# Small loads ordered behind large ones, late steps of an expert stage moved to earlier blocks, and a normalization's statistics in a pool of their own

## The chip, the cores and the metric

One core of one Trainium2 chip runs the whole layer. The metric is the device time of one execution in microseconds (us), the median of several runs. TensorE is written PE (its weight loads PEld), VectorE DVE, ScalarE ACT, GpSimd POOL, and SyncE, which only issues DMAs here, SP. L and a number is a line of the kernel before.

## The reference, cut to what matters

One decoder layer on 256 tokens of 1024 features: an RWKV-7 token mixer, then a top-4-of-32 mixture of experts, then a gated per-layer embedding, each followed by a LayerNorm of `alpha * x + sublayer(x)`.

```python
x = layer_norm(ALPHA * x + rwkv7_time_mix(x, ...), ln_mix_g, ln_mix_b)
# moe_ffn: logits -> top 4 of 32 experts per token, softmax gates; per expert e:
    hcat = xb @ w_gu[e] + b_gu[e]                       # 1024 -> 2 * 1024
    glu, lin = min(hcat[:, :F], 7), clip(hcat[:, F:], -7, 7)
    act = glu * sigmoid(1.702 * glu) * (lin + 1)
    out = act @ w_down[e] + b_down[e]                   # 1024 -> 1024, weighted by the gate
x = layer_norm(ALPHA * x + ffn, ln_ffn_g, ln_ffn_b)
ple = (p @ ple_w_proj) * sigmoid(x @ ple_w_gate + ple_b_gate)
x = layer_norm(ALPHA * x + ple, ln_ple_g, ln_ple_b)
```

Everything is float32. The expert weights alone are 32 x (8 MB + 4 MB) in HBM, and each is read once.

## The kernel before, in words

The first part (the token mixer and the router) fills about the first quarter of the span. Then comes the expert stage, `Moe.experts`, and then `Moe.tail`, which does the two last LayerNorms and the embedding.

**The ring.** The weights come through `Ring`, eleven slots of 2 MB in SBUF. `weights` writes out by hand the order in which they are loaded, `ring.plan`. The 32 experts are taken in 16 blocks b of two experts 2b and 2b+1, and a block has twelve loads of 2 MB: four of `w_gu` for the first expert, four for the second, two of `w_down` for each. I call them (b,0) to (b,11). When PE has used up a slot, `ring.free` calls `add`, which fills the slot with the next entry of the plan. So the load that is added lies one ring ahead of the one that was freed. After the last block come `wg(0)` and `wg(1)`, the weights of the embedding's gate, each in four pieces; the two `w_down` loads of expert 31 are also in four pieces each.

At entry `2 * READY - 2` (in experts; READY is 8, so before block 7) stand two entries of another kind: `ple` loads `ple_w_proj` (1 MB) and keeps its slot to the end, and `norms` only keeps a slot, into which rows are later spread over all partitions. From there on the ring has nine slots.

**Small loads.** `ring.small` is a list of loads of 4 to 64 KB that are not issued at once: each `add` takes one from it. The `ple` entry puts nine there (four pieces of `p`, four LayerNorm rows, one row `ple_b_gate`). Each even block b up to 12 puts six there: the biases of four experts, from `biases`, into the tile `raw`. In the next odd block `parts` (L1076 to L1084) splits `raw` into three bf16 parts, with two casts on ACT and three instructions on DVE, which stand behind the activation of expert 2b. All loads are issued by SP, in one order. The order of instructions on each engine comes from a scheduler that models the time of each; a small load needs no slot to come free, a large one does, and nothing ties the two together.

**A block on PE**: `gu(2b)`, `gu(2b+1)` (the products with `w_gu`, tile `ph`, L1262, closed by four bias matmuls L1210), `combine(b-1)` (tile `acc`, L1323), one step of `ready` (b from 8 to 14, seven steps that prepare the embedding and the rows; the last four are tile `pn`, L1409), the transposes `tr` (tile `ptr`, L1285) and `gates`, in even blocks from 2 on `gather(2b+2)` (tile `pg`, L1229, which picks the tokens of the next four experts into `xq`), and `down` for both experts (tile `pd`, L1310). The last block (15) has its `combine(14)` between its two `gu`, and closes with `combine(15)`, which for each half cp of the tokens adds to `acc[cp]` and then starts the embedding's product (tile `tpg`, L1330).

**The tail.** `norm(0)` takes the statistics of `acc[0]` on DVE (tile `f_st`, L1505), then `turn(0)` transposes on PE (tile `tpt`, L1520), `product(0, ...)` multiplies with `wg` (tile `tpg`, L1529); meanwhile `norm(1)` runs on DVE. Tile `f_st` lies in the tail's pool `tw`, which is opened where the experts' pool `mw` was.

Of the kernel before, what the change touches and what calls it, by code (L numbers as in the profile page):

```python
# [11 lines left out]
F32 = mybir.dt.float32  # L12
# [9 lines left out]
E = 32  # L22
KC = D // 128
# [46 lines left out]
def ln_stats(nc, pool, x, st=None):  # L70
    if st is None:
        st = pool.tile([128, 2, 6], F32, name="ln_st", bufs=2)
        for h in range(2):
            nc.vector.bn_stats(st[:, h, :], x[:, h * 512:(h + 1) * 512])
    mv = pool.tile([128, 2], F32, name="ln_mv", bufs=2)
    nc.vector.bn_aggr(mv, st)
    rs = pool.tile([128, 1], F32, name="ln_rs", bufs=2)
    rsqrt1(nc, pool, rs, mv[:, 1:2], LN_EPS)
    return mv[:, 0:1], rs
# [6 lines left out]
class Ring:  # L86


    def __init__(self, nc):
        self.nc, self.plan, self.at, self.where, self.views, self.small = nc, [], 0, {}, {}, []  # L90

    def open(self, tc, ctx):
        for i in range(RING1):
# [16 lines left out]
    def add(self, tile_):  # L110
        if self.at < len(self.plan):
            key, fill = self.plan[self.at]
            self.at += 1
            self.views[key] = fill(self.nc, tile_)
            self.where[key] = tile_

            if self.small:
                self.small.pop(0)()

    def __getitem__(self, key):  # L120
        return self.views[key]
# [2 lines left out]
        self.add(self.where[key])  # L124


def weights(A, small):

    def gu(e, i):
        def fill(nc, t):  # L130
            v = t.rearrange("p (a b) -> p a b", b=2 * D)
            nc.sync.dma_start(v, A["moe_w_gu"][0][e].rearrange("(p c) f -> p c f", c=KC)[:, 2 * i:2 * i + 2, :])  # L132
            return v
        return ("gu", e, i), fill

    def down(e, i):
        def fill(nc, t):
            v = t.rearrange("p (a b) -> p a b", b=D)
            src = A["moe_w_down"][0][e].rearrange("(h q c) d -> h q c d", h=2, c=4)[i]
            n = 4 if e == E - 1 else 1  # L140
            for k in range(n):
                ks = slice(4 // n * k, 4 // n * (k + 1))
                nc.sync.dma_start(v[:, ks], src[:, ks])
            return v
        return ("d", e, i), fill

    def ple(nc, t):
        nc.sync.dma_start(t[:, 0:2048].rearrange("p (c d) -> p c d", c=2), A["ple_w_proj"][0].rearrange("(p c) d -> p c d", c=2))
        def later(out, in_):
            small.append(lambda: nc.sync.dma_start(out, in_))  # L150
        for cp in range(2):
            o = t[:, 3072 + 256 * cp:3328 + 256 * cp]
            later(o[0:64], A["p"][0, 0, cp * 128 + 64:cp * 128 + 128, :])
            later(o[64:128], A["p"][0, 0, cp * 128:cp * 128 + 64, :])
        for i, nm in enumerate(["ln_ffn_g", "ln_ffn_b", "ln_ple_g", "ln_ple_b"]):
            later(t[i:i + 1, 2048:3072], A[nm])
        later(t[32:33, 2048:3072], A["ple_b_gate"])
        return t

    def wg(i):  # L160
        def fill(nc, t):
            v = t.rearrange("p (a b) -> p a b", b=D)
            src = A["ple_w_gate"][0].rearrange("(p c) d -> p c d", c=KC)
            for k in range(4):
                nc.sync.dma_start(v[:, k, :], src[:, 4 * i + k, :])
            return v
        return ("wg", i), fill

    plan = []
    for e in range(0, E, 2):  # L170
        if e == 2 * READY - 2:
            plan += [("ple", ple), ("norms", lambda nc, t: t)]
        plan += [gu(e + j, i) for j in range(2) for i in range(4)]
        plan += [down(e + j, i) for j in range(2) for i in range(2)]
    return plan + [wg(0), wg(1)]
# [831 lines left out]
OFF0 = 1  # L1007
OFF1 = 0
PL = 4
READY = 8  # L1010


class Moe:
# [160 lines left out]
    def experts(self, ring):  # L1174


        tc, nc, c, x1, acc = self.tc, self.tc.nc, self.c, self.x1, self.acc
        ident, gate = c["ident"], self.gate
        with ExitStack() as ctx:
            W = ctx.enter_context(tc.tile_pool(name="mw", bufs=1, side="right", reuse_waits="tile"))  # L1180
            PS = self.mps.enter_context(tc.tile_pool(name="mps", bufs=1, space=bass.MemoryType.PSUM, reuse_waits="tile"))
            xq = W.tile([128, KC, 4 * CAP], F32, name="xq")
# [36 lines left out]
            def gather(e):  # L1219
                _, oh, _ = batch(e)  # L1220
                n = min(4, E - e)
                for cp in range(2):
                    self.places(oh, e, cp)
                for q in range(KC // 2):
                    pg = bank("pg").rearrange("p (k t) -> p k t", k=2)
                    for k in range(2):
                        for cp in range(2):
                            lhs = x1[cp].rearrange("t (p c) -> t c p", c=KC)[:, 2 * q + k, :]
                            pe(nc.tensor.matmul(pg[:, k, 0:n * CAP], lhs, oh[:, cp, 0:n].rearrange("p a b -> p (a b)"),  # L1229
                                                start=cp == 0, stop=cp == 1))  # L1230
                    copy = nc.vector.tensor_copy if q % 2 else nc.scalar.copy
                    copy(xq[:, 2 * q:2 * q + 2, 0:n * CAP], pg[:, :, 0:n * CAP])
# [108 lines left out]
            for b in range(E // 2):  # L1341
                end = b == E // 2 - 1
                last = gu(2 * b)
                if b % 2 == 0 and b < E // 2 - 2:
                    ring.small += self.biases(b // 2 + 1, raw)
                elif b % 2 and not end:
                    while ring.small:
                        ring.small.pop(0)()
                    self.parts(b // 2 + 1, raw, last)
                if end:  # L1350
                    combine(b - 1)
                    tr(2 * b)
                    pgt = gates(b)
                    nc.vector.tensor_copy(GT, pgt[:, 0:T])
                gu(2 * b + 1)
                if not end:
                    if b:
                        combine(b - 1)
                    self.ready(ring, bank, b - READY, pe)
                    step()  # L1360
                    tr(2 * b)
                    pgt = gates(b)
                    nc.vector.tensor_copy(GT, pgt[:, 0:T])
                    if not b:
                        residual()
                    elif b % 2 == 0:
                        gather(2 * b + 2)
                        step()
                    tr(2 * b + 1)
                pd = [bank(f"pd{h}") for h in range(2)]  # L1370
                down(b, 0, pd)
                if end:
                    tr(2 * b + 1)
                down(b, 1, pd)
                if not b:
                    gather(2)
                    step()
# [116 lines left out]
    def tail(self, ring):  # L1494
        tc, nc, F, acc, out = self.tc, self.tc.nc, self.x1, self.acc, self.out
        ident, nm, pq = self.c["ident"], ring["norms"], ring["ple"]
        halves = [slice(512 * h, 512 * h + 512) for h in range(2)]
        with tc.tile_pool(name="tw", bufs=2, side="right", reuse_waits="tile") as W, ExitStack() as late:
            pg, xt = self.pg, [None, None]

            def norm(cp, last):
                f = F[cp]
                st = W.tile([128, 2, 6], F32, name="f_st")
                for h in range(2):
                    i = nc.vector.bn_stats(st[:, h, :], acc[cp][h])  # L1505
                    if last:
                        self.behind(i, last)
                mean, rs = ln_stats(nc, W, f, st)
                for h, hs in enumerate(halves):
                    nc.vector.scalar_tensor_tensor(f[:, hs], acc[cp][h], mean, nm[:, hs], op0=OP.subtract, op1=OP.mult)  # L1510
                return nc.vector.scalar_tensor_tensor(f, f, rs, nm[:, D:2 * D], op0=OP.mult, op1=OP.add)
# [43 lines left out]
            last = norm(0, None)  # L1555
# [25 lines left out]
def build(tc, A, out):  # L1581
    nc = tc.nc
    with ExitStack() as ctx:
        keep = ctx.enter_context(tc.tile_pool(name="keep", bufs=1))
        c = consts(tc, keep)
        x1 = [keep.tile([128, D], F32, name=f"x1_{i}") for i in range(2)]
        M = Moe(tc, keep, c, A, x1)
        M.accs, M.mps, M.pg, M.out = [ctx.enter_context(ExitStack()) for _ in range(2)], ctx.enter_context(ExitStack()), [], out
        ring = Ring(nc)
        ring.plan = weights(A, ring.small)  # L1590
        R0 = ctx.enter_context(tc.tile_pool(name="ring0", bufs=1))
        M.first(ctx.enter_context(tc.tile_pool(name="first", bufs=1, side="right")))
        rwkv(tc, ctx, ring, c, A, x1, R0, M.prepare, M.route)
        ring.more(tc, ctx)
        M.overflow()
        M.experts(ring)
        M.tail(ring)
# [15 lines left out]
```

## Time and profile before

| | |
|---|---|
| median of 3 runs | 1327.02 us (1325.14 to 1327.76) |
| the profiled execution, its own time | 1328.42 us |
| its span, first to last instruction | 1326.7 us |
| PE busy | 1204.8 us (91%) |
| DVE, ACT, POOL busy | 33%, 17%, 14% |
| HBM read | 429.50 MB |
| share of the DMA engines, loads issued by SP | 78.8% |
| chain that ended last: PE / DMA | 45% / 27% |

The profiled execution is 1.4 us above the median, and 1.7 us of its time lie outside the span. All rows below are of that execution, in us from the start of the span.

How to read it: the page divides the span into 40 slices of 33.2 us. A digit is the busy share in tenths. The line of GB/s says what the 16 DMA engines moved together. A view of windows gives the same for chosen stretches, with the clock that PE was granted (1.00 is 2.4 GHz, 0.50 is 1.2 GHz). The chain of work that ended last is followed back from the last instruction, at each step to what released it.

### The profile page before, as it was taken

How to read it: one execution, taken by the hardware profiler on the slowest of the kernel's cores; microseconds unless marked ns; L12 is line 12 of the kernel's file. 1: busy time of each engine (PE TensorE's matmuls, PEld its weight loads, DVE VectorE, ACT ScalarE, POOL GpSimd, SP SyncE). 2: the span in 40 equal slices, each digit the busy share in tenths (PEclk: the TensorE clock that was granted, in tenths of full speed). 3: DMA queues.
4: the chain of work that ended last, by engine and by line, in shares of the span. 5: the costliest groups of instructions: out<-in, count | busy, mean ns of one | idle time of the engine just before them, and what ended most of it. 6: DMA issues, size and time to landing. Idle time of an engine off the chain costs nothing.

```text
span 1326.7 us, 15094 instructions
## 1 busy us (share of the span) xinstructions
PE 1204.8 (91%) x6023; PEld 659.0 (50%) x6024; DVE 440.6 (33%) x1081; ACT 220.7 (17%) x467; POOL 180.5 (14%) x309
## 2 busy tenths in 40 slices
PE   6988788888999999999979897999899899989986
PEld 5667566776534355445425332553355255326433
DVE  5896877876212121120211110120112111110135
ACT  3554344443011010000100000100101010100001
POOL 9466545531000000000000000000000000000000
PEclk8998878897899999999999999999999999999988
DMA  7331101467699999999998999999999999999931
GB/s 216 108 116 34 32 1 33 159 270 286 231 391 426 414 427 428 414 428 428 427 415 358 431 419 426 427 428 416 429 427 426 416 428 427 429 427 427 420 134 32
DMA packets 42389, 431.58 MB, mean 325 GB/s; under 512 B 6077, under 2 KB 10629, under 8 KB 17866
## 3 DMA queue, kind: packets, MB, share of 16 engines
q1 hardware_dynamic: 41994, 430.04, 78.8%
q8 instruction: 49, 0.80, 0.2%
q10 hardware_dynamic: 320, 0.52, 0.1%
q14 instruction: 26, 0.21, 0.0%
HBM read 429.50 MB, written 1.05 MB: 325 GB/s over the span
## 4 chain that ended last, share of the span: by engine, by line
PE 45%; DMA 27%; DVE 1%; SPq 0%; issue 0%; ACT 0%; DVEq 0%; ACTq 0%
DMA ring_f<-in_moe_w_gu 24%; PE ph L1262 18%; PE pd L1310 13%; PE pg L1229 4%; PE acc L1323 4%; DMA ring_f<-in_ple_w_proj 3%; PE tpg L1529 2%; PE ptr L1285 1%; PE ph L1210 1%; PE pn L1409 1%; PE ppq L1400 1%; PE pd L1210 0%; SPq L132 0%; PE pgb L1241 0%; PE acc L1250 0%
## 5 line engine op out<-in xcount | busy, mean ns | idle before, releaser
L1262 PE MATMUL ph<-ring_f,xq 128*64 128x512 f32 x1920 | 432.4, 596 | 47.5 <-DMA ring_f<-in_moe_w_gu 47.4
L1262 PEld LDWEIGHTS ph<-ring_f,xq 128*64 128x64 f32 x1920 | 181.4, 137 | 284.0 <-issue 153.5
L1310 PE MATMUL pd<-ring_f,xg 128*64 128x512 f32 x1024 | 247.8, 596 | 0.4 <-ACT xg L1287 0.4
L1310 PEld LDWEIGHTS pd<-ring_f,xg 128*64 128x64 f32 x1024 | 93.0, 137 | 137.3 <-issue 122.2
L1275 DVE TENSOR_SCALAR g<-ph 128x512 f32<-128x512 f32 x32 | 22.1, 691 | 412.4 <-PE ph L1210 412.4
L1318 DVE COPY ob<-pd 64x512 f32<-64x512 f32 x32 | 22.0, 688 | 248.9 <-PE pd L1310 248.6
L1277 ACT ACTIVATE s<-g 128x512 f32<-128x512 f32 x32 | 20.2, 630 | 456.4 <-DVE g L1275 456.4
L1229 PE MATMUL pg<-oh,x 128*128 128x256 f32 (+1 forms) x256 | 63.5, 408 | 0.0
L1229 PEld LDWEIGHTS pg<-oh,x 128*128 128x128 f32 x256 | 61.9, 336 | 0.8 <-issue 0.8
L1323 PE MATMUL acc<-ob,oh 128*128 128x512 f32 x128 | 59.5, 606 | 0.7 <-ACT ob L1316 0.7
L1316 ACT COPY ob<-pd 128x512 f32<-128x512 f32 x16 | 9.4, 587 | 235.2 <-PE pd L1310 235.2
L369 POOL TENSOR_TENSOR w_lo<-w_raw,w_hi 128x512 fp32r<-128x512 f32 (+2 forms) x32 | 41.0, 1286 | 18.7 <-ACT w_hi L352 18.1
L1323 PEld LDWEIGHTS acc<-ob,oh 128*128 128x128 f32 x128 | 22.9, 189 | 31.0 <-issue 28.9
L352 ACT CAST w_hi<-w_raw 128x1024 fp32r<-128x1024 f32 x32 | 33.2, 1048 | 28.7 <-PE ps_p L376 15.0
L1262 PE MATMUL ph<-ring_f,xg 128*64 128x512 f32 x128 | 31.4, 644 | 2.8 <-PEq L1425 2.8
L371 DVE TENSOR_TENSOR w_lo<-w_raw,w_hi 128x512 fp32r<-128x512 f32 (+2 forms) x32 | 30.6, 960 | 9.7 <-ACT w_hi L352 8.7
L1529 PE MATMUL tpg<-ring_f,x 128*128 128x512 f32 (+1 forms) x80 | 29.4, 528 | 0.0
L1287 ACT COPY xg<-ptr 128x512 f32<-128x512 f32 x32 | 18.8, 586 | 59.6 <-PE ptr L1285 58.4
L1210 PEld LDWEIGHTS <-sel 96*64 96x64 bf16 x192 | 14.7, 110 | 23.5 <-issue 18.8
L1210 PE MATMUL ph<-B,sel 96*64 96x512 bf16 x128 | 24.9, 379 | 0.0
L1285 PEld LDWEIGHTS ptr<-ident,s 128*128 128x128 f32 x128 | 19.3, 206 | 9.7 <-issue 9.0
L1279 DVE TENSOR_TENSOR s<-s,l 128x512 f32<-128x512 f32 x32 | 22.1, 692 | 3.9 <-ACT s L1277 0.7
(357 smaller groups left out, 1469.5 us busy)
## 6 DMA issues: line engine op xcount, KB each, us to landing
ring_f<-in_moe_w_gu SPq DMA_DIRECT2D x128, 2048.0 KB
ring_f<-in_moe_w_down SPq DMA_DIRECT2D x62, 2048.0 KB
w_raw<-in_rwkv_w_rkv SPq DMA_DIRECT2D x24, 512.0 KB
w_raw<-in_rwkv_w_o SPq DMA_DIRECT2D x8, 512.0 KB
ring_f<-in_moe_w_down SPq DMA_DIRECT2D x8, 512.0 KB
ring_f<-in_ple_w_gate SPq DMA_DIRECT2D x8, 512.0 KB
x<-in_x SPq DMA_DIRECT2D x4, 256.0 KB
ring_f<-in_ple_w_proj SPq DMA_DIRECT2D x1, 1024.0 KB
```

The source lines that it names most:

```text
L352: eng.copy(out, in_)
L369: nc.gpsimd.tensor_sub(lw[:, D - g:], raw[:, D - g:], hi.bitcast(F32)[:, D - g:])
L371: nc.vector.tensor_sub(lw[:, 0:D - g], raw[:, 0:D - g], hi.bitcast(F32)[:, 0:D - g])
L1210: pe(nc.tensor.matmul(out, self.sel3[0:96, r:r + 1].to_broadcast([96, CAP]), self.B[e // 4 % 2], start=start, stop=stop))
L1229: pe(nc.tensor.matmul(pg[:, k, 0:n * CAP], lhs, oh[:, cp, 0:n].rearrange("p a b -> p (a b)"), start=cp == 0, stop=cp == 1))
L1262: pe(nc.tensor.matmul(ph[n][64 * h:64 * h + 64, :], xg[:, k, i * CAP:i * CAP + CAP], w[:, k % 2, o:o + 512], start=k == 0, stop=False))
L1275: nc.vector.tensor_scalar(g, ph[0], 7.0, None, op0=OP.min)
L1279: return i, nc.vector.tensor_mul(s, s, l)
L1285: pe(nc.tensor.transpose(pt[:, k, :], av[:, k, :], ident))
L1310: pe(nc.tensor.matmul(pd[h][side[h], :], actT[:, i, k, 64 * fh:64 * fh + 64], ring["d", e, fh][:, k, 512 * h:512 * h + 512], start=False, ...
L1323: pe(nc.tensor.matmul(acc[cp][h], GT[:, cp * 128:cp * 128 + 128], ob[:, h], start=False, stop=2 * b == E - 2, skip_group_check=True))
L1529: i = nc.tensor.matmul(pg[cp][o // 512][:, o % 512:o % 512 + n], xt[cp][:, k, :], ring["wg", k // 4][:, k % 4, o:o + n], start=False, stop ...
```

## The change

- `add` ties each small load behind the large load that was issued last (`behind` is an ordering on the queue, without a semaphore).
- READY goes from 8 to 6: the entries `ple` and `norms` stand before block 5, and the seven steps of `ready` are done in blocks 6 to 12.
- `gather(30)`, the last one, is done in block 13 in place of block 14. The others stay.
- The statistics of `norm` (tile `f_st` and the small tiles of `ln_stats`) go to a pool `tn` of their own, which is opened ahead of `mw`.

```diff
@@ class Ring
             if self.small:
-                self.small.pop(0)()
+                self.behind(self.small.pop(0)(), self.last[0])
@@
-def weights(A, small):
+def weights(A, small, last):
+
+    def load(nc, out, in_):
+        last[:] = [nc.sync.dma_start(out, in_)]
 
     def gu(e, i):
         def fill(nc, t):
             v = t.rearrange("p (a b) -> p a b", b=2 * D)
-            nc.sync.dma_start(v, A["moe_w_gu"][0][e].rearrange("(p c) f -> p c f", c=KC)[:, 2 * i:2 * i + 2, :])
+            load(nc, v, A["moe_w_gu"][0][e].rearrange("(p c) f -> p c f", c=KC)[:, 2 * i:2 * i + 2, :])
             return v
...
-READY = 8
+READY = 6
@@ def experts
+            self.N = self.small.enter_context(tc.tile_pool(name="tn", bufs=1, side="right", reuse_waits="tile"))
             W = ctx.enter_context(tc.tile_pool(name="mw", bufs=1, side="right", reuse_waits="tile"))
@@
                     if not b:
                         residual()
-                    elif b % 2 == 0:
-                        gather(2 * b + 2)
+                    elif b % 2 == 0 and 2 * b + 6 < E or b == E // 2 - 3:
+
+                        gather(E - 2 if b % 2 else 2 * b + 2)
                         step()
@@ def tail
             def norm(cp, last):
                 f = F[cp]
-                st = W.tile([128, 2, 6], F32, name="f_st")
+                st = self.N.tile([128, 2, 6], F32, name="f_st", bufs=2)
...
-                mean, rs = ln_stats(nc, W, f, st)
+                mean, rs = ln_stats(nc, self.N, f, st)
```

The loads of `w_down`, `ple_w_proj` and `ple_w_gate` go through `load` in the same way as the one shown.

## Rows read from the trace of the kernel before

**Rows 1.** The page: the span, and the line of GB/s in 40 slices of 33.2 us.

```profile
span 1326.7 us, 15094 instructions
...
GB/s 216 108 116 34 32 1 33 159 270 286 231 391 426 414 427 428 414 428 428 427 415 358 431 419 426 427 428 416 429 427 426 416 428 427 429 427 427 420 134 32
```

**Rows 2.** Windows over the expert stage. Columns: stretch and its length, busy time (and number of instructions) of PE, PEld, DVE, ACT, POOL, then PE's granted clock, DMA share, GB/s.

```profile
365.00:716.00 351.00, 341.78 (x1538) 163.50 (x1535) 63.73 (x111) 28.78 (x48) 0.00 (x0) 1.00 1.00 420
731.00:1184.60 453.60, 415.34 (x1818) 190.19 (x1813) 69.34 (x119) 36.60 (x62) 0.00 (x0) 1.00 1.01 425
1184.60:1253.00 68.40, 68.40 (x288) 35.47 (x290) 8.90 (x16) 5.53 (x10) 0.00 (x0) 0.98 1.00 425
```

**Rows 3.** The chain that ended last, from the last `gu` load of block 14 to the end of block 15, pieces in order of time: start, length, what.

```profile
1184.60 3.65 PE ph L1262 x16
1188.69 3.63 PE acc L1323 x8
1192.32 1.91 PE pn L1409 x4
...
1195.13 7.61 PE pg L1229 x32
...
1203.53 9.51 PE pd L1310 x30
...
1254.19 6.87 PE pd L1310 x32
...
1262.46 7.14 PE pd L1310 x32
```

**Rows 4.** The timeline of SP's issues, the last of `w_down` and the last of the gate's weights (start, length of the issue, line, what), and a row of who waited for whom on SP over the whole span (us in total, times, longest).

```profile
1253.75 0.33 SPq L143 DMA_DIRECT2D ring_f<-in_moe_w_down  x1
...
1263.99 0.33 SPq L165 DMA_DIRECT2D ring_f<-in_ple_w_gate  x1
...
SPq L165 <- DMA ring_f<-in_moe_w_down: 7.1, 8, 0.9
```

**Rows 5.** SP's issues around the entry `ple`, and the window of PE alone in which the DMA engines ran low (columns: PE busy, granted clock, DMA share, GB/s).

```profile
686.87 0.33 SPq L148 DMA_DIRECT2D ring_f<-in_ple_w_proj  x1
691.76 0.24 SPq L150 DMA_DIRECT2D ring_f<-in_ln_ffn_g  x1
...
724.63 0.24 SPq L150 DMA_DIRECT2D ring_f<-in_ple_b_gate  x1
...
717.00:727.00 10.00, 10.00 (x41) 1.00 0.61 210
```

**Rows 6.** Windows in which loads of biases passed through the DMA engines (same columns): four loads, two, five, one after the five, five, one after the five; and the stretch around the first six loads.

```profile
557.00:561.00 4.00, 4.00 (x22) 1.00 1.03 365
552.00:555.00 3.00, 3.00 (x18) 1.00 1.03 388
790.00:793.00 3.00, 1.20 (x6) 1.00 1.04 355
794.00:800.00 6.00, 4.51 (x24) 1.00 0.99 418
908.00:912.00 4.00, 4.00 (x22) 1.00 1.00 344
912.00:919.00 7.00, 6.31 (x30) 1.00 1.01 425
340.00:350.00 10.00, 7.17 (x22) 0.66 0.09 21
```

**Rows 7.** `parts` in block 3: the timelines of ACT and DVE (start, length, line, what, and in brackets the idle time before it).

```profile
527.18 0.60 ACT L1076 CAST B<-raw 96x512 bf16<-96x512 f32 x1
...
530.73 0.42 DVE L1083 CAST B<-raw 32x512 bf16<-32x512 f32 x1
540.09 0.69 DVE L1275 TENSOR_SCALAR g<-ph 128x512 f32<-128x512 f32 x1 [8.95 <-PE ph L1210]
```

**Rows 8.** The timeline of PE at the start of block 14.

```profile
1153.04 10.74 PE L1262 MATMUL ph<-ring_f,xq 128*64 128x512 f32 x48
1165.03 3.65 PE L1262 MATMUL ph<-ring_f,xq 128*64 128x512 f32 x16 [1.25 <-DMA ring_f<-in_moe_w_gu]
```

**Rows 9.** The chain at the start of the tail.

```profile
1270.27 1.98 PE acc L1323 x4
1272.26 1.91 PE tpg L1330 x4
1274.17 1.93 PE acc L1323 x4
...
1276.17 1.31 DVE f_st L1505 x2
...
1282.53 1.97 PE tpt L1520 x8
1284.51 8.45 PE tpg L1529 x16
1292.95 0.88 PE tpt L1520 x8
```

**Rows 10.** PE's granted clock in two stretches of it (windows, columns as in Rows 2).

```profile
1278.00:1280.50 2.50, 0.00 (x0) 0.00 (x0) 2.29 (x8) 0.00 (x0) 0.00 (x0) 1.00 0.00 0
1284.50:1287.30 2.80, 2.80 (x5) 1.25 (x5) 2.52 (x11) 0.59 (x1) 0.00 (x0) 0.50 0.00 0
```

More of the change, by code (lines that the diff above doesn't have):

```diff
@@ L89, in __init__ @@
     def __init__(self, nc):
-        self.nc, self.plan, self.at, self.where, self.views, self.small = nc, [], 0, {}, {}, []
+        self.nc, self.plan, self.at, self.where, self.views, self.small, self.last = nc, [], 0, {}, {}, [], []
     def open(self, tc, ctx):
@@ L142, in fill @@
                 ks = slice(4 // n * k, 4 // n * (k + 1))
-                nc.sync.dma_start(v[:, ks], src[:, ks])
+                load(nc, v[:, ks], src[:, ks])
             return v
@@ L147, in ple @@
     def ple(nc, t):
-        nc.sync.dma_start(t[:, 0:2048].rearrange("p (c d) -> p c d", c=2), A["ple_w_proj"][0].rearrange("(p c) d -> p c d", c=2))
+        load(nc, t[:, 0:2048].rearrange("p (c d) -> p c d", c=2), A["ple_w_proj"][0].rearrange("(p c) d -> p c d", c=2))
         def later(out, in_):
@@ L164, in fill @@
             for k in range(4):
-                nc.sync.dma_start(v[:, k, :], src[:, 4 * i + k, :])
+                load(nc, v[:, k, :], src[:, 4 * i + k, :])
             return v
@@ L1589, in build @@
         ring = Ring(nc)
-        ring.plan = weights(A, ring.small)
+        ring.plan = weights(A, ring.small, ring.last)
+        ring.behind = M.behind
         R0 = ctx.enter_context(tc.tile_pool(name="ring0", bufs=1))
@@ L1594, in build @@
         ring.more(tc, ctx)
+        M.small = ctx.enter_context(ExitStack())
         M.overflow()
```

## The prediction

> **What bounds the kernel now.** PE is busy 91% of the span and leads the chain, so it looks like the bound. Read the GB/s line first: from about 390 us to 1260 us it stands at 414 to 428 in every slice but one [rows 1]. The windows say the same: 420 and 425 GB/s over 800 us, while PE leaves 38 us of the second stretch idle [rows 2]. PE's busy share is high only because the loads come about as fast as it can use them. A 2 MB load (2.097 MB) takes 2.097/0.428 = 4.9 us, and the four steps of PE that use it about 3.65 us; PE then waits 1.25 us for the next [rows 8]. So in the middle the time is bytes by rate, and PE work moved there is free while the loads go on.
>
> The end is different. From 1184.60, where the last `gu` load of block 14 has landed (call this moment L), the chain is PE almost alone to 1269.60, which is L + 85.0 [rows 3]. But the loads are not far ahead. SP's last eight issues, the pieces of `wg`, each wait for a piece of `w_down` of expert 31, and there are eight of those [rows 4]: at most eight loads are under way, and the last issue at 1263.99 tells that the last `w_down` piece landed then, at L + 79.4. What PE can gain at the end is cut off there. Last, the tail: two chains, PE and DVE, with a gap in which PE does nothing [rows 9].
>
> **The change part by part.** The sum is made of differences, so I take it from the median, 1327.0 (the profiled execution has 1328.4).
>
> *Last blocks.* Block 14 loses its `pn` step (1.91) and `gather(30)` (7.61) [rows 3]. It also loses something that the diff does not name: `down` takes 9.51 for its first 30 records after a gather, where a block without one has 6.87 for 32 [rows 3], so 2.6 more. In all 12.1 us of PE work. The loads don't let all of it through. Counted from L, 16 loads are still to come, four `down`, eight `gu`, four `down`; the last `gu`, the twelfth, lands at 12 x 4.9 = 58.8. PE then needs 4.1 (1184.60 to 1188.69), until 62.9. The second `down` load of expert 30 landed when SP issued the last `w_down` piece, eight issues on, at 1253.75 = L + 69.2 [rows 4]. Half a `down` is 3.4, to 72.6; the last transpose and its copy take 1261.06 to 1262.46 = 1.4, to 74.0; `down` of expert 31 takes 6.87 to 7.14 [rows 3], to 80.9. The loads alone would allow 79.4 + 0.9 for the last quarter = 80.3. I take 80.9, against 85.0 now: **4.1 us**. Bounds 3 and 4.7.
>
> What hides the gather in block 13: it adds 7.61 + 2.6 there and loses a `pn`, 8.3 us net. PE began `gu` of block 14 at 1153.04 and waited for loads from 1163.8 on [rows 8]. Starting at 1161.3, its eight loads at 3.43 end at 1188.8 and the biases at 1189.2, 0.5 us later than now, and PE waits again at the next `gu`. Without that cover the whole 8.3 would come back. The later freed slots cost nothing as long as under eight loads x 4.9 = 39 us are missing.
>
> *READY.* The seven steps move two blocks ahead and two slots leave the ring 24 loads sooner. Nine slots carry 425 GB/s, eleven carried 420 [rows 2]: no loss, and the steps fall beside waits of PE. Zero; if nine slots did not do, the steps and the `ple` loads would show as a dip below 420 between 560 and 680 us.
>
> *The ties.* Now SP issues `ple_w_proj` at 686.87 and then the nine small loads in a row, one for each load that lands, up to 724.63 [rows 5]. With at most eight under way, the small ones crowd the large ones out: from 717 to 727 the rate is 210 GB/s. Against 428 that is (1 - 210/428) x 10 = 5.1 us lost. With a large load between any two small ones, four large ones (19.6 us of work) stay under way, and this hole closes. The small loads still cost something in a full queue. Four of them lose (1 - 365/428) x 4 = 0.59 us, two 0.28, five 0.51 and 0.78: 0.10 to 0.16 each, mean 0.14 to 0.15; one alone 0.14 and 0.05 [rows 6]. Let c be this price once each is apart. 36 loads of biases pay 0.15 each today, 5.4 us in all; the first six pay nothing, since they pass at 343 to 346 us, where the rate is 21 GB/s [rows 6], and will now come in the full stream. So the stream changes by 51c - 5.4 - 5.1. I take c = 0.14, between the lone and the grouped rows: 7.1 - 10.5 = **-3.4 us**. Bounds c = 0.05 and c = 0.25 (the dearest row and half more): -8.0 and +2.3.
>
> The ties add a wait. `parts` in an odd block now waits for small loads that land later; on ACT the activation of expert 2b+1 and the copy of the transposes stand behind it, on DVE the clamps, and PE's `down` waits for them. The sixth bias is tied to the load added at the sixth step after it, which is (b,6) with nine slots. It lands 4.9 us before the last `gu` load, PE is done 4.1 later, and `parts` takes 4.0 (527.18 to 531.15) [rows 7]: 5 us to spare. In block 5 the nine `ple` loads stand ahead and the last bias falls behind (6,0): PE could be held some 26 us there, against four loads (19.6 us) that already have slots. PE makes up 1.25 us on every load afterwards. Zero, up to 6.
>
> A rule speaks against the ties. The Trainium skill, "DMA: Bandwidth & Descriptors", section "Bandwidth", tells to batch loads to 1 MiB and calls transfers under 64 KB descriptor-dominated; its table has 0.68 us for 4 KB and 0.95 us for 64 KB. By that c would be about 0.8, an estimate, and the ties would cost 41 - 10.5 = 30 us instead of gaining 3. The rows of grouped loads above have a sixth of it, with other loads under way on the same engines.
>
> *norm's pool.* `acc[0]` is complete when its second pair of matmuls ends, at 1272.26, but `f_st` starts at 1276.17, just after the matmuls of `acc[1]`, which it doesn't read (1276.10) [rows 9]. What it shares with them is the ground: its tile lies where the experts' tiles were, one of which (`ob`) those matmuls read. In a pool of its own it starts at 1272.3, 3.9 sooner; the first half could start half a matmul pair earlier, 4.5 in all, and there PE's own `tpg`, done at 1278.0, stops it. I take **4.2 us** (3.8 to 4.5).
>
> *PE's clock.* PE does nothing from 1278.0 to 1282.53; the granted clock is still 1.00 until 1280.5 and 0.50 from then to 1287.3 [rows 9, 10], 2.4 and 1.2 GHz. So the 8 transposes take 1.97 and not 0.88 to 1.04, of which half lies on the path (the product starts after four), and the next 16 records 8.45; 64 later ones show what they cost at 2.4 GHz, 6.9. With the gap down to under 1 us the clock should stay: 0.5 + 1.6 = **2.1 us** (0 to 2.5).
>
> Sum: 4.1 + 3.4 + 4.2 + 2.1 = 13.8; 1327.0 - 13.8 = **1313.2 us**.
>
> **The rivals.** As a function of c the time is 1327.0 - 4.1 - 4.2 - 2.1 - 10.5 + 51c = 1306.1 + 51c.
>
> A, slower: a small load costs per interruption of the large stream, not per load. Then every one of the 51 pays what a whole group pays now, 0.51 to 0.78 [rows 6], mean 0.65, and the time is 1306.1 + 33 = 1339. It decides from c = 0.46 on (1329.7). Against it: two cost 0.28, four 0.59, so the price goes with the number. This is also the direction in which the skill's table points; with its figures the time would be 1347, an estimate. Chance 0.06.
>
> B, the wait in the tail is not the pool's: `f_st` still starts after `acc[1]`, and the clock falls as before. 1313.2 + 6.3 = 1319.5. For it: the row names only PE. Against it: the only other thing that the two share is the order on PE. Chance 0.13.
>
> C, the ties don't do what they say, because SP's order around the large loads stays such that the hole remains or is paid elsewhere, by a late `parts` for instance: no gain on the stream, 1316.6, with up to 6 lost in block 5, 1322. Chance 0.15.
>
> D, the loads set the end already, and the last blocks give nothing (the second `down` load of expert 30 lands later than I counted): 1317.3. Chance 0.06.
>
> **How the numbers follow.** The forecast has 0.60. A measurement of this kernel tells 0.2%, 2.7 us, from no change. Faster by more: 0.60 + 0.12 of B + 0.10 of C + 0.05 of D = 0.87; the rest of B, C and D, where two of them meet, is within 0.2%: 0.07; A is slower: 0.06. The range goes from c = 0.05 with the other terms as taken (1308.6) to B with c = 0.18 at its top, 1306.1 + 6.3 + 9.2 = 1321.6: 1308.5 to 1321.5.
>
> **What would show it.** Right: no slice under 410 GB/s between 400 and 1250 us, and the issues of small loads each behind one of 2 MB; PE waiting for loads in block 15's `gu`, which it doesn't now; the end of the last `down` at L + 81; `f_st` under 3 us after the end of the last `down`; granted clock 1.00 through the first product. Wrong: a late `parts` seen as idle ACT before L1076 and PE idle before `pd` in odd blocks; an odd block 13 that ends more than 8 us later against the loads; a clock of 0.50 that only moves to another place in the tail.

## The result, and the profile after

The changed kernel takes 1316.94 us (median of 8 runs, 1313.58 to 1321.29) against 1326.78 us (8 runs, 1323.08 to 1328.19) for the kernel before in the same job: ratio 0.9932, 95% interval 0.9915 to 0.9949, so 9.0 us faster by the ratio. The forecast was 1313.2 with a range of 1308.5 to 1321.5: the time lies in the range, 3.7 us above the forecast. Three of the four terms came out as worked out; the one for the ties did not come at all.

The page of the changed kernel, its span and its GB/s in 40 slices (32.9 us each), beside [rows 1]:

```profile
span 1315.1 us, 15081 instructions
...
GB/s 228 99 117 33 33 1 33 161 264 296 213 378 423 426 428 416 427 429 407 420 421 428 416 427 427 426 416 427 428 421 424 426 428 416 428 428 427 424 225 32
```

The slice of 358 is gone; the lowest is 407, at the `ple` loads, which now pass two blocks earlier. So the forecast's sign for the ties ("no slice under 410") is met but for one slice by 3. Yet the time did not follow. PE's windows of the same stretches (columns: stretch and length, PE busy, granted clock, DMA share, GB/s), beside [rows 2, 5]:

```profile
365.00:716.00 351.00, 336.48 (x1517) 1.00 1.00 418
731.00:1184.60 453.60, 431.90 (x1873) 0.99 1.01 424
1184.60:1253.00 68.40, 60.81 (x276) 1.00 1.00 424
717.00:727.00 10.00, 10.00 (x40) 1.00 1.01 431
600.00:610.00 10.00, 10.00 (x42) 1.00 1.02 393
```

The window of 210 GB/s is a full one (431), and where the `ple` loads stand now it is 393. In the third stretch PE is idle for 7.6 us, where before it was busy all the time: the last blocks are bound by the loads now. The timeline of PE in block 15 shows it, each step of `gu` of expert 30, the last one of expert 31 and both of `down` of expert 30 waiting for their load (start, length, line, what, in brackets the idle time):

```profile
1207.82 3.65 PE L1266 MATMUL ph<-ring_f,xq 128*64 128x512 f32 x16 [1.32 <-DMA ring_f<-in_moe_w_gu]
1212.62 3.65 PE L1266 MATMUL ph<-ring_f,xq 128*64 128x512 f32 x16 [1.15 <-DMA ring_f<-in_moe_w_gu]
...
1251.87 3.65 PE L1314 MATMUL pd<-ring_f,xg 128*64 128x512 f32 x16 [1.32 <-DMA ring_f<-in_moe_w_down]
```

The chain that ended last, beside [rows 3, 9]:

```profile
1132.89 7.63 PE pg L1233 x32
...
1141.33 9.51 PE pd L1314 x30
...
1212.95 38.87 DMA ring_f<-in_moe_w_down
1251.87 3.65 PE pd L1314 x16
...
1256.93 7.14 PE pd L1314 x32
...
1266.77 0.71 DVE f_st L1510
...
1272.54 0.73 PE tpt L1525 x4
...
1273.97 7.13 PE tpg L1534 x16
1281.11 0.88 PE tpt L1525 x8
```

`gather(30)` (`pg`) and the long `down` behind it (9.51) stand in block 13; a transfer of 38.87 us stands in the chain where `pn`, `pg` and `down` stood. `f_st` is no longer one piece of two records behind both halves of `acc`: its first record runs at 1265.91, 1.8 us after the end of the last `down`. The first 16 records of the product take 7.13 where they took 8.45.

**One caution before numbers of two profiles are subtracted.** The expert stage doesn't begin at the same moment. Its first `ph` record starts at 342.93 in the profile of before and at 341.11 in that of after; over all profiles of this study, whose first part is the same work, it lies between 337.6 and 343.4. So I count each profile from its first `ph`. From there the last `w_down` piece lands (start of SP's last issue, as in [rows 4]) at 921.06 before and 920.91 after; the last `down` ends at 926.62 and 922.91; PE's last product (tile `tpg`, both halves) ends at 971.5 and 961.5. Of these 10.0 us, 3.7 come up to the end of `down`, and 6.3 in the tail. The loads themselves end where they ended.

### The profile page after: what moved, and what is told of

The parts are those of the page before. It is cut to its first block, busy times and chain, and to the rows that moved or that the text cites. A ratio compares the mean times of both kernels' runs of the same rounds, so it can differ in the third digit from the quotient of the medians.

```text
span 1315.1 us, 15081 instructions
## 1 busy us (share of the span) xinstructions
PE 1202.0 (91%) x6023; PEld 663.7 (50%) x6024; DVE 442.1 (34%) x1081; ACT 220.8 (17%) x467; POOL 179.1 (14%) x309
## 4 chain that ended last, share of the span: by engine, by line
PE 38%; DMA 34%; DVE 1%; issue 0%; ACT 0%; DVEq 0%; SPq 0%; ACTq 0%
DMA ring_f<-in_moe_w_gu 21%; PE ph L1266 16%; DMA ring_f<-in_moe_w_down 13%; PE pd L1314 11%; PE pg L1233 3%; PE acc L1327 3%; PE tpg L1534 2%; PE ptr L1289 1%; PE pn L1414 1%; PE ph L1214 1%; PE pd L1214 0%; PE pgb L1245 0%; PE acc L1254 0%; PE ppq L1405 0%; PE pgt L1300 0%
## 5 line engine op out<-in xcount | busy, mean ns | idle before, releaser
L1266 PEld LDWEIGHTS ph<-ring_f,xq 128*64 128x64 f32 x1920 | 185.1, 137 | 271.8 <-issue 143.6
L355 ACT CAST w_hi<-w_raw 128x1024 fp32r<-128x1024 f32 x32 | 33.2, 1048 | 29.7 <-issue 13.6
```

The source lines that it names most:

```text
L355: eng.copy(out, in_)
L1266: pe(nc.tensor.matmul(ph[n][64 * h:64 * h + 64, :], xg[:, k, i * CAP:i * CAP + CAP], w[:, k % 2, o:o + 512], start=k == 0, stop=False))
```

## The experiments

"By the ratio" below is the ratio times 1326.5 us. The runs of each group shared a chip and the runs of the kernel before.

**One part at a time.** In the first group T says that the ties bring about nothing, R that they bring what was forecast.

The change without the ties:

```diff
-                self.behind(self.small.pop(0)(), self.last[0])
+                self.small.pop(0)()
```

> The changed kernel without the ties alone (small loads are issued where the scheduler puts them; READY 6, the gather and the pool stay). Theory T, the trailing DMA engine: a load is there when the slowest of the 16 engines has landed its part, and the hole in the GB/s after the ple loads is mostly the other engines waiting for it; so the ties are worth under 1.5 us: 1316 to 1318.5 against 1316.9 with ties, with the hole back near 600 us. Theory R, the prediction's: the hole is lost time of the whole stream, the ties are worth 3.4 us, and the 4 us that are missing were lost elsewhere: 1320.3.

Measured: 1314.45 us, ratio 0.9920 (0.9900 to 0.9941). Not slower than with the ties.

Only the ties (READY back to 8, gathers and pool as before):

> The kernel before with the ties alone. T: 1325.5 to 1327.5 against 1326.8, no slice under 400 GB/s in the stream, and yet the last w_down piece lands at most 1 us sooner. R: 1323.4, and the last w_down piece lands 3.4 us sooner.

Measured: 1328.08 us, ratio 1.0012 (0.9999 to 1.0025): +1.6 us by the ratio, forecast -3.4. Both runs speak for T.

Only the pool of the statistics:

> The kernel before with the pool of norm's statistics alone. T and R alike: f_st starts 3.8 to 4.5 us sooner after the end of the last down, the clock stays at 1.00 in the tail, together 6.3 us: 1320.5. If the gain is the gather's or the ties', 1326.8.

Measured: 1318.03 us, ratio 0.9951 (0.9934 to 0.9969): -6.5 us. In its chain `f_st` is a single record again, at 1268.18, with the end of `down` at 1265.49:

```profile
1258.35 7.14 PE pd L1311 x32
1268.18 0.71 DVE f_st L1506
1273.94 0.73 PE tpt L1521 x4
1275.37 7.13 PE tpg L1530 x16
```

Only READY 6 and the moved gather:

```diff
-READY = 8
+READY = 6
-                    elif b % 2 == 0:
-                        gather(2 * b + 2)
+                    elif b % 2 == 0 and 2 * b + 6 < E or b == E // 2 - 3:
+                        gather(E - 2 if b % 2 else 2 * b + 2)
```

> The kernel before with READY 6 and the gather in block 13 alone. T: the end of the last down comes 3.5 us sooner against the landing of the last w_down piece, READY is free: 1323.2. R, with the missing time lost in block 13 or by the ring of nine slots from block 4 on: 1325.5 to 1327.

Measured: 1320.90 us, ratio 0.9975 (0.9961 to 0.9990): -3.3 us. In its chain the last `down` ends at 1260.40, 1.9 us after the last `w_down` piece landed (1258.46; 5.6 us before), but `f_st` comes 6.6 us after it, as before, and the product is long (8.73):

```profile
1253.26 7.14 PE pd L1310 x32
1266.97 1.31 DVE f_st L1506 x2
...
1275.31 8.73 PE tpg L1530 x16
```

The parts add up: -6.5 - 3.3 + 1.6 = -8.2, against -9.0 for the whole. What is left to explain is why a closed hole gave nothing.

**What a small load costs.** In the second group T says that a load has landed only when the slowest of its DMA engines is done, so that the price must be taken there (0.24 us when apart); M is the price of the prediction, a mean over the engines.

The changed kernel without the loads of the biases of experts 4 to 31 (42 small loads left out; these experts add stale biases):

```diff
-                    ring.small += self.biases(b // 2 + 1, raw)
+                    pass
```

> The changed kernel without the 42 small loads that bring the biases of experts 4 to 31 during the stream (their rows are left out, so these experts add stale biases; the nine ple loads stay, tied). T (a load counts as landed when the slowest of the 16 DMA engines has its part, and a small load that stands alone costs that engine about 0.24 us): 42 x 0.24 = 10 us less than the changed kernel, about 1307. M (the price is the mean over the engines, 0.14 to 0.16, as the prediction had it): 42 x 0.15 = 6.3 us less, about 1310.5. Under 4 us less would speak against both.

Measured: 1306.00 us, ratio 0.9851 (0.9837 to 0.9864): 10.7 us less than the changed kernel by the ratios, 0.26 us for each load. T.

Each load of `b_down` with 16 rows:

> The changed kernel, but each load of b_down takes 16 rows instead of 8 (the later 8 are not used), so that it is spread over as many DMA engines as the load of b_gu. T (only the work of the slowest engine counts; spreading does not relieve it): within 1 us of the changed kernel, 1316 to 1318. S (that the engines drift apart costs time by itself, as the marks of one load then come up to 9 us apart): less drift, 1 to 3 us faster, 1314 to 1316.

Measured: 1320.98 us, ratio 0.9965 (0.9951 to 0.9978): 4.4 us slower than the changed kernel by the ratios. S falls: the engines did drift less (6.2 us at the end where the changed kernel has 9.1, see below), and it was not faster. T misses as well, since it expected no change; the rows that were added seem to cost something. In a list of landings as the one below, its batches of six took 1.2 us more in all. The profiled run, 1317.0, was the fastest of its five, and its last piece lands 921.2 us after the first `ph`, as in the changed kernel; the rest of the 4.4 stays open.

Each batch of biases loaded once, two loads in place of six, and copied on POOL:

```diff
-                for r in range(3) for i, src in enumerate(["moe_b_gu", "moe_b_down"])]
+                for r in range(1 if n else 3) for i, src in enumerate(["moe_b_gu", "moe_b_down"])]
...
+                    for r in (1, 2):
+                        nc.gpsimd.tensor_copy(raw[32 * r:32 * r + 32], raw[0:32])
                     self.parts(b // 2 + 1, raw, last)
```

> The changed kernel, but each batch of biases is loaded once (two small loads instead of six) and copied on POOL to the two other groups of partitions: 28 small loads fewer in the stream, 14 copies of 32x512 more on POOL, which is idle there. T: 28 x 0.24 = 6.7 us less than the changed kernel, about 1310. M: 28 x 0.15 = 4.2 us less, about 1312.7. If the copies come late and hold up the biases: no gain.

Measured: 1309.07 us, ratio 0.9868 (0.9853 to 0.9884): 8.5 us less than the changed kernel by the ratios, and the fastest complete version of the study. The copies cost POOL 9.1 us in all, in time in which it waited for the biases (groups of instructions: busy time, mean ns of one, idle time before):

```profile
L1354 POOL COPY raw<-raw 32x512 f32<-32x512 f32 x14 | 9.1, 648 | 742.6 <-DMA raw<-in_moe_b_down 742.2
```

The same without the ties:

> As the run before it, and without the ties (the version that should beat both kernels). T (in a group a small load costs the slowest engine 0.14): 28 x 0.14 = 3.9 us less than the changed kernel without ties (1314.5), about 1310.5, so no slower and hardly faster than the tied form. R (a group of small loads is one interruption and costs the same with two as with six): 1313.5 to 1314.5.

Measured: 1310.87 us, ratio 0.9892 (0.9876 to 0.9908). The interval, 1310.0 to 1314.3 us by the ratio, holds T's time and R's; against R speaks that the last piece lands sooner than with all 51 small loads (914.65 us after the first `ph`, 920.5 and 920.7 in the two runs without ties). Against the two runs of the changed kernel without ties (0.9920 above, 0.9927 below) it is 3.7 to 4.6 us less, 0.13 to 0.17 for each of the 28 loads. Against the form with the ties it is 3.2 us slower by the ratios, and at first sight the ties now help. But the intervals overlap, and the two profiled executions don't decide it: this one, the fastest of its four, took 1309.29 us, the one with the ties, the slowest of its four, 1310.41. Counted from the first `ph`, the last piece lands only 0.65 us later without them (914.65 and 914.00), and 1.7 us more go in the tail, where the product's first 16 records took 8.83 and not 7.13 (see the clock below).

**With and without ties, side by side.** From these four kernels I had worked out a gain of 7.1 us for the hole and a price of 0.17 us for each load that is set apart. The third group tests that.

The changed kernel again, and without the ties again:

> The changed kernel itself, beside the next three. 1316 to 1318 as before, if nothing but the kernels makes the differences; near 1320 would say that runs of one kernel differ by this much and that the run with sixteen rows is no slower than the changed kernel.

Measured: 1317.47 us, ratio 0.9934 (0.9916 to 0.9952), as the first time.

> The changed kernel without the ties, again, beside the changed kernel. T (ties gain H by closing the hole at the ple loads and pay 0.17 more for each of 51 small loads; from the four kernels with 51 and 23 small loads, H is 7.1): 51 x 0.17 - 7.1 = 1.6 us faster than the changed kernel. P (the prediction: ties gain 3.4): 3.4 us slower.

Measured: 1316.14 us, ratio 0.9927 (0.9913 to 0.9941): 0.9 us faster than with the ties, with intervals that overlap widely. P falls.

Only the nine `ple` loads tied:

```diff
-                self.behind(self.small.pop(0)(), self.last[0])
+                one = self.small.pop(0)
+                i = one()
+                if hasattr(one, "tied"):
+                    self.behind(i, self.last[0])
```

> The changed kernel with only the nine small ple loads tied, the biases free. T: the hole closes (7.1) for nine times 0.17: 5.6 us faster than without any tie, 7 us faster than with all, about 1310. P (price per small load the same apart or in a group, 0.14): as the changed kernel. Q (the hole is no loss, since the leading engines only wait there for the one that is behind): as the kernel without ties.

Measured: 1317.02 us, ratio 0.9928 (0.9914 to 0.9943). T in this form misses by 5.7 us, and the 7.1 falls with it: closing the hole alone gave nothing that can be measured. The windows show that it was closed (first without ties, then with these nine):

```profile
600.00:610.00 10.00, 10.00 (x40) 1.00 0.75 274
600.00:720.00 120.00, 104.32 (x463) 1.00 0.98 412
```

```profile
600.00:610.00 10.00, 10.00 (x40) 1.00 1.03 388
600.00:720.00 120.00, 105.40 (x468) 1.00 1.01 419
```

By the bytes the second is 1.7% ahead over 120 us, 2 us; the last piece lands 0.9 us sooner (919.8 against 920.7 after the first `ph`); and the tail took 1.4 of it back, with a product of 8.51 for its first 16 records.

Both together, one load in three and only the nine tied:

> Each batch of biases loaded once and copied on POOL (14 small loads in the stream), these free, the nine ple loads tied. T: 14 x 0.17 = 2.4 us faster than with the 14 tied too (1309.0 against the kernel before at 1326.5), about 1306.6. P: no faster than that, 1309.

Measured: 1309.61 us, ratio 0.9884 (0.9867 to 0.9901). By the times that is not faster than with all tied. Its profile leans the other way: the last piece lands 911.75 us after the first `ph`, 2.25 us sooner than with all tied (914.00), which is near T's 2.4. The intervals of the two overlap, so what it costs to tie the biases stays open by some 2 us. What makes the versions fast is the number of small loads. Counted from the first `ph`, the last piece lands sooner with 28 loads fewer in every form: by 5.9 us without ties, 6.9 with all tied and 8.1 with the nine tied (0.21, 0.25 and 0.29 for each), and by 10.0 us with 42 fewer (0.24).

## Why the prediction was right, and where it was wrong

**Last blocks, 4.1: right.** The end of the last `down`, counted from the first `ph`, came 3.7 us sooner in the changed kernel and 4.1 in the run of this part alone (922.5 against 926.6); timed, the part gave 3.3. The limit is the one that was named: `down` ends 2.0 us after the last piece of `w_down` lands (1264.07 and 1262.02), where 5.6 us passed before. The cover for the gather held too: block 14 starts its `gu` 7.0 us later than before, counted from the first `ph` (1158.21 in its profile), and PE still waits for loads from 1206 on. Rival D falls.

**norm's pool, 4.2, and the clock, 2.1: right, together 6.3 against 6.5 timed.** From the end of `down` to the first transpose it was 13.0 us in each profile without the pool and is 8.5 in each with it: 4.5. From there to the end of the product it was 31.9 (31.2 and 32.2 in the two other profiles without the pool) and is 30.1 in nine of the eleven profiles with it: 1.1 to 2.1. Rival B falls. The clock is the less certain of the two (last section).

**READY, zero: right, as far as the runs tell.** Nine slots from block 5 on carry 424 GB/s, and with READY 6 and the gather alone the last piece lands 920.6 us after the first `ph`, where before it was 921.1. The sign that was named against it, a dip below 420 GB/s between 560 and 680 us, did come (407), but the `ple` loads stand there now, which made a dip of their own where they stood before (358); no run moved one without the other.

**The wait behind the ties, zero: right, though it came, and in part by luck.** The sign of a late `parts` is there: ACT stood idle before its first cast in five blocks, in all 20.1 us, where before it never did. PE did not wait for it: its idle time before `pd` that ends with ACT's copy `xg` is 0.4 us in both kernels (first the timeline of ACT in block 7, where the wait was longest, then the last lines on ACT's instructions that write `B` and on PE's that write `pd`):

```profile
760.18 0.62 ACT L1079 CAST B<-raw 96x512 bf16<-96x512 f32 x1 [6.05 <-DMA raw<-in_moe_b_down]
...
  DMA raw<-in_moe_b_down: 20.1, 5
...
  ACT xg L1291: 0.4, 1
```

Block 5, for which the prediction feared 26 us, is the place of the luck. The scheduler put the casts there at 670.54, behind the second activation (648.94) and the copies `xg` (652.59), so that they could hold up neither; the wait was 1.2 us. The reason that the prediction gave, PE making up the time afterwards, was not put to the test.

**The ties on the stream, -3.4: wrong.** With the ties the time was 1.6 us longer in the kernel before, and 1.6 and 0.9 us longer in the two comparisons of the changed kernel, none of it clear of zero; that is inside the bounds of the term (-8.0 to +2.3). The step that failed is "the stream changes by 51c - 5.4 - 5.1", in two of its terms, and both for one reason: they were read from GB/s, the sum of 16 engines, while PE waits for a load until the slowest engine has finished its part. The trace's records of semaphore updates show that: each load gives 16 marks, and the first and the last lie 1.9 us apart at the start of the stage, and 4.4 (before) or 9.1 us (changed kernel) at its end. I call this the drift. The following list is worked out from the last mark of each load: how much more than 4.89 us passed between the last marks of two large loads, summed by what lay between them, over the stretch from 360 to 1237 us; for the `ple` group the 2.45 us of its own 1 MB are taken off. (Sums of single steps, good to some 0.5, since a step beside a group can be put into one row or another.)

```
us beyond 4.89 per 2 MB load          before   ties only   changed
up to 393 us, and the first 6 biases     5.6         6.9       6.8
the other 36 biases                      7.8         8.3       7.9
the 9 small ple loads                    5.2         2.7       3.7 (with the first fetch)
steps at three fetches of code           2.8         5.4       3.6 (the other two)
the rest                                 2.4         1.6       2.1
sum                                     23.8        24.9      24.1
```

Read from it:

(1) The price c, on the slowest engine, is 7.8 to 8.3 for 36, 0.22 to 0.23 each, and by the landings it is the same in a group (before) as apart (ties). The windows of [rows 6] gave 0.14, because the engines ahead went on moving bytes while the last was late. The times of the runs with fewer small loads lie around it: 10.7 us for 42 is 0.26, 8.5 for 28 is 0.30, 5.8 for the same 28 with only the `ple` loads tied is 0.21, and without any tie it is 0.13 to 0.17. The intervals, some 2 us each way, are too wide to tell these apart.

(2) The hole, 5.1 by its bytes, was worth 2.5 at most: in it the engines that were ahead ran dry while the slowest worked on, and the drift fell from 3.4 to 0.6 us. The loads of the changed kernel never let the engines come together again. It may be worth less: 1.3 of the 5.2 is the step right behind the hole, which goes with a fetch of code (736.0, see 4). And among the kernels with READY 6, where one fetch falls into the group in each, the group costs 5.0 to 5.3 without ties (three profiles) and 3.8 to 4.0 with the nine or all loads tied (three profiles): 1.0 to 1.5 for the hole.

(3) The first six biases, which passed free, cost 1.2 now, 0.8 by the forecast's c.

(4) Not in the forecast at all: the instruction queue (q8) fetches 16 KB of the program every 30 us, 30 times from 360 us on. Most of these leave no step; every eighth does, at 608.3, 862.8 and 1113.7 us in the changed kernel and within 5 us of these in before; a fourth, at 384.1 (385.7 before), goes with a step of 1.7 (1.4) in the first row of the list. At the two later ones the step is 1.9 and 1.7 in the changed kernel, 2.0 and 1.9 with the ties alone, and 0.2 and 1.0 before. Before has steps four fetches further on instead, 1.3 at 736.0 and 0.9 at 992.0, and so has the run with the pool alone (1.5 and 0.9). The hole by itself does not explain that: the three kernels with READY 6 and no ties have it too, and their two later steps are 1.2 to 1.7. That every eighth fetch falls on one and the same engine, and makes a step when this engine is the last one, is argued from these times and was not tried.

The Trainium skill, "DMA: Bandwidth & Descriptors", section "Why a DMA increments its semaphore by 16 and not by 1", says that the engines of one load finish independently and that only all 16 counts mean that the data are there, and that a load with fewer rows than 16 uses only the lowest-numbered engines. The marks agree with the first and with the number of engines: a load of `b_down`, 8 rows, has eight marks that come as its data land and one about 0.5 us after its issue, a row of the LayerNorms or the gate one of each. With 16 rows for `b_down` the drift at the end was 6.2 and not 9.1 us. But the short loads are not its main source: without any load of biases it is still 6.6, and of its growth from 1.9 to 9.1 us in the changed kernel 4.9 come in the three steps at fetches. That the last engine is one of the low-numbered ones no record here shows.

**Rivals.** C, the ties don't help the stream, is what happened to this term (1316.6 was its time, 1316.94 is the measured one), though not by its mechanism: the order on SP was as the diff says, and the hole did close. The changed kernel's issues, each small load behind one of 2 MB:

```profile
598.77 0.33 SPq L130 DMA_DIRECT2D ring_f<-in_moe_w_gu  x1
601.82 0.25 SPq L153 DMA_DIRECT2D ring_f<-in_ln_ffn_g  x1
602.16 0.33 SPq L130 DMA_DIRECT2D ring_f<-in_moe_w_gu  x1
602.55 0.28 SPq L153 DMA_DIRECT2D ring_f<-in_ln_ffn_b  x1
```

A, a price for each interruption (c of 0.46 or more), falls: apart or grouped, a small load costs 0.13 to 0.30 by the times and 0.21 to 0.29 by the landings. (The prediction reads the line of [rows 1] as 414 to 428 GB/s; it goes up to 431, and nothing hangs on that.)

## What to carry to other kernels

In a stream bound by its loads, take prices from the times at which loads land, not from GB/s: a dip in the rate can be the engines that are ahead waiting for the last one, and filling it then gives little (1.0 to 2.5 us here, where the bytes said 5.1). The number of small loads counts, some 0.25 us each here by the landings; what their place is worth was too little to time. To load a thing once and copy it on an idle engine (8.5 us here) beat every order of the same loads. And before two profiles are subtracted, set both to a common event: here the start of the stage alone varied by 6 us.

## What the runs showed of the hardware that was not expected

**The engines drift apart and stay apart** as long as the queue never runs dry: up to 9.1 us between the first and the last mark of one load in the changed kernel, with GB/s still at 427. It grows most at every eighth fetch of the program: from 2.6 to 4.2, from 5.1 to 6.9 and from 7.7 to 9.2 us.

**A full clock is not sure even with PE busy.** The granted clock was to stay at 1.00 (2.4 GHz) once the gap ahead of the first transposes was short. It did in nine of the eleven profiles with the pool; in two it fell to 0.50 (1.2 GHz) for 3.4 us in the same place, with the same instructions ahead of it (windows of PE, first of the changed kernel, then of the one with only the `ple` loads tied):

```profile
1272.50:1274.00 1.50, 1.19 (x9) 1.00 0.00 0
1274.00:1276.00 2.00, 2.00 (x5) 1.00 0.00 0
```

```profile
1271.80:1273.20 1.40, 1.34 (x8) 0.78 0.00 0
1273.20:1275.00 1.80, 1.79 (x2) 0.50 0.00 0
```

It costs 1.4 to 1.7 us of the tail when it happens. What sets it off stays open.
